# Pinning each engine to the staggered program order, and eight instead of six x and output buffers, in a matmul-mask-softmax kernel

## The chip, the cores and the metric

The kernel runs on one core of one Trainium2 chip. The metric is the device time of one execution in microseconds (us). A profiled execution also has a span, from its first to its last instruction, which is some 2 us shorter than the time. Executions of the kernel before fall into two groups: about 108.7 us, with a mean granted TensorE clock of 0.93, and about 110.8 us, with 0.91. (The granted clock is the share of its full clock that the profile records for TensorE.) Runs over 1.5% above the fastest of the same kernel are called slow. In the lines of the profile PE is TensorE, PEld its weight loads, DVE is VectorE, ACT ScalarE, POOL GpSimd and SP the engine that issues the transfers; L104 is line 104 of that kernel.

## The reference

```
batch, m, k, n = 16, 512, 512, 512
y = scale * np.matmul(x, weight)            # scale = 0.125
y = np.where(mask == 1, y, -1e9)            # mask = 1 strictly below the diagonal
y_max = np.max(y, axis=-1, keepdims=True)
y_exp = np.exp(y - y_max)
return (y_exp / np.sum(y_exp, axis=-1, keepdims=True)).astype(np.float32)
```

Sixteen batches of 512x512 in float32 are read and written: 1.049 MB in and 1.049 MB out for each. The weight and four diagonal blocks of the mask are read once.

## The kernel before

A batch goes through six steps. `load` fetches x. `cast` makes it bf16 on VectorE. `transpose` turns it on TensorE, by sixteen 128x128 transposes into PSUM, and evicts one half on VectorE and one on ScalarE. `multiply` makes four row tiles on TensorE, adds the mask through a matmul with the identity, and takes the exponential with its row sum on ScalarE. `normalise` multiplies by the reciprocal of the sums on VectorE. `store` writes out. `X_BUFS` and `OUT_BUFS` say how many x tiles (`xf`) and output tiles (`ot`) there are to take turns with; `xb` is x in bf16, `pt` its transpose in PSUM, `xt` the evicted transpose, `py` the product in PSUM. A tile framework makes the semaphores, and its scheduler may reorder the instructions of each engine.

```python
X_BUFS = 6
OUT_BUFS = 6
...
    def transpose(b):
        xb = st_xb.pop(b)
        xt = xt_pool.tile([P, KT, QT, P], BF16, name="xt")
        for half in range(2):
            pt = psum_t.tile([P, 2, QT, P], BF16, name="pt")
            for kk in range(2):
                ...                                   # eight transposes into pt
            if half == 0:
                nc.vector.tensor_copy(xt[:, 0:2], pt)  # "eviction"
            else:
                nc.scalar.copy(xt[:, 2:4], pt)
        st_xt[b] = xt
...
    for i in range(B + 1):
        if i + 2 < B:
            cast(i + 2)
        if i + 1 < B:
            transpose(i + 1)
        if i < B:
            multiply(i)
        if i >= 1:
            normalise(i - 1)
            store(i - 1)
            if i - 1 + X_BUFS < B:
                load(i - 1 + X_BUFS)
```

The softmax here doesn't subtract the row's maximum and nothing guards it: scores larger than these inputs give would overflow.

## Time and profile before

| | before |
|---|---|
| time, first three runs | 108.56, 110.81, 110.86 us (median 110.81) |
| span of the profiled execution | 106.9 us |
| bytes moved | 34.87 MB |
| busy: TensorE / VectorE / ScalarE | 68% / 53% / 50% |
| granted TensorE clock, mean | 0.932 |

No engine is near full, and the transfers move at 400 GB/s or more in 23 of the 40 slices and fall off in the last quarter. The prediction below shows the slices, the waits and one turn of the timeline. One line more is of use, from the waits of the queue that issues the transfers. Its columns are: who waits for whom, total us, times, longest us.

```profile
SPq L139 <- DVE ot L135: 77.7, 16, 8.5
```

All sixteen stores stand waiting for a normalisation. The longest wait, 8.5 us, is natural: it is that of the first store, before any batch is done. But after 50 us the queue still waits 46.1 us in eight times, up to 7.3 us for one store, when no load is late.

### The profile page before, as it was taken

To read this page: it belongs to the slowest core of one execution; us is meant where nothing else is said; L and a number is where in the kernel's file an instruction comes from. 1 tells how busy PE (TensorE), PEld (TensorE's weight loads), DVE (VectorE), ACT (ScalarE), POOL (GpSimd) and SP (SyncE) were. 2 spreads that over 40 slices of the span, in tenths; PEclk is the share of its full clock that TensorE was granted. 3 is DMA by queue.
4 is the path that set the end of the run, shared out by engine and by line. 5 is a ranking of instruction groups with operands and counts; after the bars stand their busy time and mean duration, and the time that the engine had idled before them with its cause. 6 is when DMAs were issued, how large, how long until landed. Compare 5 with 4: busy or idle time off the path is not lost. (4 is left out here: it accounts for less than half of the span.)

```text
span 106.9 us, 1599 instructions
## 1 busy us (share of the span) xinstructions
PE 73.2 (68%) x576; PEld 48.2 (45%) x576; DVE 57.0 (53%) x116; ACT 53.6 (50%) x147; POOL 14.9 (14%) x36
## 2 busy tenths in 40 slices
PE   0026994999999998937749669392992939929100
PEld 0025563685687665535535445362551626526000
DVE  0067329768987767788290390928409366070510
ACT  4007263696886874835613836375353563355300
POOL 7990001010410110110010100101001010010100
PEclk9999999999999999999975999999579996799975
DMA  2998999999999999999999999999950724505354
GB/s 28 400 382 282 422 417 411 406 411 417 369 296 371 415 400 420 415 420 418 418 423 420 415 418 418 420 425 420 412 204 14 294 98 193 199 0 239 153 222 170
DMA packets 9814, 34.95 MB, mean 327 GB/s; under 512 B 592, under 2 KB 1104, under 8 KB 9808
## 3 DMA queue, kind: packets, MB, share of 16 engines
q1 hardware_dynamic: 9808, 34.87, 82.4%
q8 instruction: 4, 0.07, 0.2%
q14 instruction: 2, 0.02, 0.0%
HBM read 18.09 MB, written 16.78 MB: 326 GB/s over the span
## 5 line engine op out<-in xcount | busy, mean ns | idle before, releaser
L104 PE MATMUL py<-w_bf,xt 128*128 128x256 bf16 (+1 forms) x256 | 56.6, 355 | 17.0 <-DVE xt L90 17.0
L119 ACT ACTIVATE ot<-py 128x256 f32<-128x256 f32 (+1 forms) x64 | 31.2, 491 | 31.5 <-PE py L111 31.0
L104 PEld LDWEIGHTS <-xt 128*128 128x128 bf16 x256 | 25.9, 105 | 33.8 <-DVE xt L90 19.2
L135 DVE TENSOR_SCALAR ot<-ot,rinv 128x256 f32<-128x256 f32 (+1 forms) x64 | 25.2, 438 | 1.6 <-issue 0.5
L77 DVE CAST xb<-xf 128x2048 bf16<-128x2048 f32 x16 | 20.1, 1257 | 7.4 <-DMA xf<-in_x_dram 7.4
L88 PE MATMUL pt<-ident_bf,xb 128*128 128x128 bf16 x256 | 17.8, 225 | 9.1 <-DVE xb L77 9.1
L88 PEld LDWEIGHTS <-xb 128*128 128x128 bf16 x256 | 16.0, 101 | 11.8 <-DVE xb L77 10.6
L132 DVE RECIPROCAL rinv<-rsum 128x4 f32<-128x4 f32 x16 | 2.8, 176 | 32.9 <-ACT ot L119 32.9
L92 ACT COPY xt<-pt 128x1024 bf16<-128x1024 bf16 x16 | 16.2, 1013 | 7.5 <-PE pt L88 4.0
L136 POOL MEMSET ot<- 1x256 f32 x16 | 7.8, 484 | 85.6 <-DVE ot L135 85.6
L111 PE MATMUL py<-diag_bf,ident_bf 128*128 128x256 bf16 x64 | 18.8, 294 | 0.0
L119 ACT ACTIVATION_READ_ACCUMULATOR ot<-py 128x1 f32 x64 | 12.7, 199 | 0.0
L90 DVE COPY xt<-pt 128x1024 bf16<-128x1024 bf16 x16 | 10.9, 680 | 1.5 <-PE pt L88 1.5
L111 PEld LDWEIGHTS <-ident_bf 128*128 128x128 bf16 x64 | 6.8, 106 | 5.1 <-issue 1.4
L168 ACT CAST w_bf<-w_f 128x512 bf16<-128x512 f32 x2 | 1.2, 622 | 6.7 <-DMA w_f<-in_weight_dram 6.7
L159 POOL MEMSET ot<- 128x512 f32 x6 | 3.0, 520 | 0.1
L160 POOL MEMSET ot<- 1x256 f32 x6 | 2.7, 481 | 0.0
L168 ACT ACT_TABLE_LOAD x1 | 1.3, 1283 | 0.7 <-PEq L208 0.7
L166 DVE CAST w_bf<-w_f 128x512 bf16<-128x512 f32 x2 | 0.8, 424 | 1.4 <-DMA w_f<-in_weight_dram 1.4
L170 DVE TENSOR_SCALAR diag_bf<-diag_f 64x512 bf16<-64x512 f32 x2 | 0.8, 416 | 0.0
L157 POOL MEMSET diag_bf<- 64x512 bf16 x1 | 0.5, 520 | 0.1
L156 POOL MEMSET diag_bf<- 64x512 bf16 x1 | 0.5, 523 | 0.0
(6 smaller groups left out, 0.9 us busy)
## 6 DMA issues: line engine op xcount, KB each, us to landing
xf<-in_x_dram SPq DMA_DIRECT2D x16, 1024.0 KB, 12.7
out_dram<-ot SPq DMA_DIRECT2D x16, 1024.0 KB, 9.2
w_f<-in_weight_dram SPq DMA_DIRECT2D x1, 1024.0 KB, 7.5
diag_f<-in_mask_dram SPq DMA_DIRECT2D x4, 64.0 KB, 6.7
```

What stands on the lines that cost most here:

```text
L77: nc.vector.tensor_copy(xb, st_x.pop(b))
L88: nc.tensor.transpose(pt[:, kk, q], xb[:, q, kt * P : (kt + 1) * P], ident_bf)
L90: nc.vector.tensor_copy(xt[:, 0:2], pt)
L92: nc.scalar.copy(xt[:, 2:4], pt)
L104: nc.tensor.matmul(py[:, :NC], lhsT=xt[:, kt, q], rhs=w_bf[:, kt, :NC], start=(kt == 0), stop=(kt == KT - 1),)
L111: nc.tensor.matmul(py[:, h * HB : NC], lhsT=ident_bf, rhs=diag_bf[:, q], start=False, stop=True, skip_group_check=True,)
L119: nc.scalar.activation(out=ot[:, q, :NC], in_=py[:, :NC], func=AF.Exp, bias=0.0, scale=float(scale), accum_out=rsum[:, q : q + 1],)
L132: nc.vector.reciprocal(rinv, st_sum.pop(b))
L135: nc.vector.tensor_scalar_mul(ot[:, q, :NC], ot[:, q, :NC], rinv[:, q : q + 1])
L136: nc.gpsimd.memset(ot[0:1, 0, :HB], 1.0 / N)
L159: nc.gpsimd.memset(ot[:, 0:2, HB:], 0.0)
L160: nc.gpsimd.memset(ot[0:1, 0, HB:], 1.0 / N)
```

## The change

The intent is to fix the order of every engine's instructions to the order of the program text, so that the scheduler can't move them. The pin is `keep_in_program_order`, which puts an instruction behind the one traced before it on the same engine. The text separates the evictions from the transposes, and both sets of buffers grow to eight.

```diff
-X_BUFS = 6
-OUT_BUFS = 6
+X_BUFS = 8
+OUT_BUFS = 8
...
+    seq = tc.keep_in_program_order
...
-        nc.vector.tensor_copy(xb, st_x.pop(b))
+        seq(nc.vector.tensor_copy(xb, st_x.pop(b)))
...                                   (the same seq(...) around every transfer, matmul,
...                                    activation, reciprocal, multiply and memset of a batch)
+    def evict(b):
         xt = xt_pool.tile([P, KT, QT, P], BF16, name="xt")
-        ... (transposes and evictions of each half in turn)
+        pt = st_pt.pop(b)
+        seq(nc.vector.tensor_copy(xt[:, 0:2], pt[0]))
+        seq(nc.scalar.copy(xt[:, 2:4], pt[1]))
         st_xt[b] = xt
...
     for i in range(B + 1):
+        if i + 1 < B:
+            transpose(i + 1)
         if i + 2 < B:
             cast(i + 2)
         if i + 1 < B:
-            transpose(i + 1)
+            evict(i + 1)
         if i < B:
             multiply(i)
```

More of the change, by code (lines that the diff above doesn't have):

```diff
@@ L66 @@
     ots = [const.tile([P, QT, N], FP32, name=f"ot{i}") for i in range(OUT_BUFS)]
-    st_x, st_xb, st_xt, st_sum = {}, {}, {}, {}
+    st_x, st_xb, st_pt, st_xt, st_sum = {}, {}, {}, {}, {}
+    seq = tc.keep_in_program_order
     def load(b):
         xf = x_pool.tile([P, QT, K], FP32, name="xf")
-        nc.sync.dma_start(xf.rearrange("p (h s) k -> p h (s k)", h=2), x_r[b])
+        seq(nc.sync.dma_start(xf.rearrange("p (h s) k -> p h (s k)", h=2), x_r[b]))
         st_x[b] = xf
@@ L81, in transpose @@
         xb = st_xb.pop(b)
-        xt = xt_pool.tile([P, KT, QT, P], BF16, name="xt")
-        for half in range(2):
-            pt = psum_t.tile([P, 2, QT, P], BF16, name="pt")
-            for kk in range(2):
-                kt = 2 * half + kk
-                for q in range(QT):
-                    nc.tensor.transpose(pt[:, kk, q], xb[:, q, kt * P : (kt + 1) * P], ident_bf)
-            if half == 0:
-                nc.vector.tensor_copy(xt[:, 0:2], pt)
-            else:
-                nc.scalar.copy(xt[:, 2:4], pt)
+        st_pt[b] = [psum_t.tile([P, 2, QT, P], BF16, name="pt") for _ in range(2)]
+        for kt in range(KT):
+            for q in range(QT):
+                seq(
+                    nc.tensor.transpose(
+                        st_pt[b][kt // 2][:, kt % 2, q],
+                        xb[:, q, kt * P : (kt + 1) * P],
+                        ident_bf,
+                    )
+                )
+    def evict(b):
+        xt = xt_pool.tile([P, KT, QT, P], BF16, name="xt")
+        pt = st_pt.pop(b)
+        seq(nc.vector.tensor_copy(xt[:, 0:2], pt[0]))
+        seq(nc.scalar.copy(xt[:, 2:4], pt[1]))
         st_xt[b] = xt
@@ L103, in multiply @@
             for kt in range(KT):
-                nc.tensor.matmul(
-                    py[:, :NC],
-                    lhsT=xt[:, kt, q],
-                    rhs=w_bf[:, kt, :NC],
-                    start=(kt == 0),
-                    stop=(kt == KT - 1),
-                )
-            nc.tensor.matmul(
-                py[:, h * HB : NC],
-                lhsT=ident_bf,
-                rhs=diag_bf[:, q],
-                start=False,
-                stop=True,
-                skip_group_check=True,
-            )
-            nc.scalar.activation(
-                out=ot[:, q, :NC],
-                in_=py[:, :NC],
-                func=AF.Exp,
-                bias=0.0,
-                scale=float(scale),
-                accum_out=rsum[:, q : q + 1],
+                seq(
+                    nc.tensor.matmul(
+                        py[:, :NC],
+                        lhsT=xt[:, kt, q],
+                        rhs=w_bf[:, kt, :NC],
+                        start=(kt == 0),
+                        stop=(kt == KT - 1),
+                    )
+                )
+            seq(
+                nc.tensor.matmul(
+                    py[:, h * HB : NC],
+                    lhsT=ident_bf,
+                    rhs=diag_bf[:, q],
+                    start=False,
+                    stop=True,
+                    skip_group_check=True,
+                )
+            )
+            seq(
+                nc.scalar.activation(
+                    out=ot[:, q, :NC],
+                    in_=py[:, :NC],
+                    func=AF.Exp,
+                    bias=0.0,
+                    scale=float(scale),
+                    accum_out=rsum[:, q : q + 1],
+                )
             )
@@ L131, in normalise @@
         rinv = sum_pool.tile([P, QT], FP32, name="rinv")
-        nc.vector.reciprocal(rinv, st_sum.pop(b))
+        seq(nc.vector.reciprocal(rinv, st_sum.pop(b)))
         for q in range(QT):
             NC = (q // 2 + 1) * HB
-            nc.vector.tensor_scalar_mul(ot[:, q, :NC], ot[:, q, :NC], rinv[:, q : q + 1])
-        nc.gpsimd.memset(ot[0:1, 0, :HB], 1.0 / N)
+            seq(nc.vector.tensor_scalar_mul(ot[:, q, :NC], ot[:, q, :NC], rinv[:, q : q + 1]))
+        seq(nc.gpsimd.memset(ot[0:1, 0, :HB], 1.0 / N))
     def store(b):
-        nc.sync.dma_start(out_r[b], ots[b % OUT_BUFS].rearrange("p (h s) n -> p h (s n)", h=2))
+        seq(nc.sync.dma_start(out_r[b], ots[b % OUT_BUFS].rearrange("p (h s) n -> p h (s n)", h=2)))
     load(0)
-    nc.sync.dma_start(w_f32, weight.rearrange("(kt p) n -> p kt n", p=P))
+    seq(nc.sync.dma_start(w_f32, weight.rearrange("(kt p) n -> p kt n", p=P)))
     for h in range(2):
@@ L147 @@
             r = h * HB + g * P
-            nc.sync.dma_start(
-                diag_f32[g * HP : (g + 1) * HP, 2 * h : 2 * h + 2],
-                mask[r : r + P, r : r + P].rearrange("(p s) c -> p s c", s=2),
+            seq(
+                nc.sync.dma_start(
+                    diag_f32[g * HP : (g + 1) * HP, 2 * h : 2 * h + 2],
+                    mask[r : r + P, r : r + P].rearrange("(p s) c -> p s c", s=2),
+                )
             )
@@ L163 @@
     transpose(0)
+    evict(0)
     for kt in range(KT):
         if kt % 2 == 0:
-            nc.vector.tensor_copy(w_bf[:, kt], w_f32[:, kt])
+            seq(nc.vector.tensor_copy(w_bf[:, kt], w_f32[:, kt]))
         else:
-            nc.scalar.copy(w_bf[:, kt], w_f32[:, kt])
+            seq(nc.scalar.copy(w_bf[:, kt], w_f32[:, kt]))
     for g in range(2):
-        nc.vector.tensor_scalar(
-            out=diag_bf[g * HP : (g + 1) * HP, :, g * P : (g + 1) * P],
-            in0=diag_f32[g * HP : (g + 1) * HP],
-            scalar1=-MASK_NEG,
-            scalar2=MASK_NEG,
-            op0=ALU.mult,
-            op1=ALU.add,
+        seq(
+            nc.vector.tensor_scalar(
+                out=diag_bf[g * HP : (g + 1) * HP, :, g * P : (g + 1) * P],
+                in0=diag_f32[g * HP : (g + 1) * HP],
+                scalar1=-MASK_NEG,
+                scalar2=MASK_NEG,
+                op0=ALU.mult,
+                op1=ALU.add,
+            )
         )
```

## The prediction

> **What bounds the kernel now.** I began with the page's slices, because they show at once that there are two regimes.
>
> ```profile
> PE   0026994999999998937749669392992939929100
> DVE  0067329768987767788290390928409366070510
> PEclk9999999999999999999975999999579996799975
> DMA  2998999999999999999999999999950724505354
> GB/s 28 400 382 282 422 417 411 406 411 417 369 296 371 415 400 420 415 420 418 418 423 420 415 418 418 420 425 420 412 204 14 294 98 193 199 0 239 153 222 170
> ```
>
> A slice is 106.9 / 40 = 2.67 us. Up to slice 29 (about 78 us) the DMA engines run at 400 to 425 GB/s, but for a dip to 296 in slices 10 to 12. In the last 29 us the rate is mostly below 240. The windows view gives the means (columns: busy us and instructions of each engine, granted TensorE clock, DMA share, GB/s):
>
> ```profile
> 26.00:34.00 8.00, 8.00 (x75) 5.81 (x72) 6.94 (x15) 5.97 (x19) 1.77 (x2) 1.00 0.98 344
> 34.00:54.00 20.00, 16.16 (x142) 10.74 (x140) 13.08 (x30) 13.09 (x38) 2.10 (x5) 1.00 1.02 416
> 54.00:74.00 20.00, 13.98 (x108) 9.25 (x108) 10.56 (x23) 9.80 (x27) 1.34 (x3) 0.91 1.02 419
> 77.50:107.00 29.50, 15.96 (x115) 9.78 (x113) 10.91 (x25) 11.18 (x31) 1.79 (x4) 0.85 0.41 162
> ```
>
> The waits then say who holds up whom (total us, times, longest):
>
> ```profile
> DVE rinv L132 <- ACT ot L119: 32.9, 13, 4.2
> PE py L104 <- DVE xt L90: 17.0, 10, 1.9
> DVE xb L77 <- DMA xf<-in_x_dram: 7.4, 2, 5.7
> ```
>
> The casts wait for a load only twice, for the first two batches. So no later load is late: compute runs behind the loads, the loads (six buffers deep) are finished at 78 us, and five batches are left to compute with nothing to load. One period of that tail in the timeline (start us, busy us, instruction, idle before):
>
> ```profile
> 82.29 0.83 PE L104 MATMUL py<-w_bf,xt 128*128 128x256 bf16 x6 [1.93 <-DVE xt L90]
> ...
> 85.34 1.06 PE L88 MATMUL pt<-ident_bf,xb 128*128 128x128 bf16 x16
> 85.54 0.60 ACT L119 ACTIVATE ot<-py 128x512 f32<-128x512 f32 x1 [0.28 <-PE py L111]
> ...
> 86.53 1.14 DVE L135 TENSOR_SCALAR ot<-ot,rinv 128x256 f32<-128x256 f32 x3
> ...
> 87.60 0.67 DVE L90 COPY xt<-pt 128x1024 bf16<-128x1024 bf16 x1
> 88.19 0.47 DVE L135 TENSOR_SCALAR ot<-ot,rinv 128x512 f32<-128x512 f32 x1
> 88.33 0.86 PE L104 MATMUL py<-w_bf,xt 128*128 128x256 bf16 x6 [1.93 <-DVE xt L90]
> ```
>
> The multiply starts at 82.29, the next batch's transposes stand behind it, and VectorE takes reciprocal and three normalising multiplies of the old batch before it evicts the new transposes at 87.60. Only then can the next multiply start, at 88.33. This ring is 88.33 - 82.29 = 6.04 us per batch, with 1.9 us of idle TensorE. **The bound is an ordering ring, not an engine.**
>
> **What the Trainium skill says.** "Perfetto Trace Analysis", section Optimization Strategy, says that a kernel can have several regimes with a different most-contended engine, and that interleaving the regimes can help. The trace agrees: 416 to 419 GB/s for forty microseconds, then 162. "DMA: Bandwidth & Descriptors", section Where 436 GB/s comes from, puts the ceiling of a core's transfers at 435 GB/s. The saturated windows here hold 414 to 419, so I use the measured rates. "TensorE: Matmul & The Clock Gate", Part 1, says that TensorE has a full and a half clock, chosen by activity over windows of about 3.4 us, idleness giving the half clock. The trace has both: the clock row falls to 5, and the ring then lasts longer (next multiply at 96.04, so 7.71 us). But the longest wait of the multiplies is 1.9 us, so here less than a fully idle window was enough. The same Part 1 says that VectorE and ScalarE queues are strictly first in, first out, which is why program order matters; the ring above, where an eviction stands behind a normalisation, agrees.
>
> **The change, part by part.** No arithmetic is added. Two ot buffers add two 128x512 memsets of 0.52 us and two small ones on GpSimd, before first use and off the path.
>
> *Order.* Each turn becomes, on TensorE: transposes of i+1, multiply of i; on VectorE: cast of i+2, eviction of i+1, normalisation of i-1; on ScalarE: eviction of i+1, exponentials of i. The instruction order of the built kernel shows just this on every engine. Multiply i now needs only an eviction of the turn before, so the ring is cut. What remains is each engine's own work. The trace already has a stretch where the scheduler chose nearly such an order:
>
> ```profile
> 26.62 0.60 PE L104 MATMUL py<-w_bf,xt 128*128 128x256 bf16 x4
> ...
> 30.55 0.60 PE L104 MATMUL py<-w_bf,xt 128*128 128x256 bf16 x4
> ```
>
> That is 30.55 - 26.62 = 3.93 us per batch with TensorE always busy: 16 transposes from 29.66 to 30.55 (0.89) and a multiply of about 3.04. VectorE starts its pieces in that stretch at distances of 0.61 (eviction), 0.20 (reciprocal), 1.46 (normalise) and 1.15 (cast), in all 3.42. ScalarE has 1.01 for its eviction, 2 x 0.37 and 2 x 0.58 for exponentials, in all 2.9. So compute can go at 3.93 us per batch. The DMA needs 2 x 1.049 MB / 417 GB/s = 5.03 us per batch. **DMA becomes the bound.**
>
> *Buffers.* The dip of slices 10 to 12 comes when six loads have landed and stores are still few (the second store is issued at 26.12). With eight x buffers two more loads, 2 x 2.5 = 5 us of transfer, stand in the queue. The second load lands at 12.64 (its cast waits for it); six more at 2.54 us bring the eighth to about 27.9. When is the first store? Turn 0 now puts the transposes of batch 1 first: cast 12.64 to 13.87, transposes at the cold clock 1.9 us to 15.8, multiply 0 some 4 us (half cold) to 19.8, transposes of batch 2 to 20.7, eviction 21.4, normalisation 1.8, store at about 23.4. That is 5 us later than the 18.24 of before, but ahead of 27.9, so the queue does not run dry.
>
> *The sum.* From the slices, 2.67 x (28 + 400 + 382 + 282) kB plus 1.95 us at 422 GB/s, 3.74 MB have moved by 12.64 us. In all 34.87 MB must move (18.09 read, 16.78 written). Up to the last load: 34.87 - 3.74 - 8 stores of 1.049 = 22.74 MB at 416 GB/s = 54.7 us, so 67.3. Then eight stores alone, 8.39 MB. A lone store shows 401 to 410 GB/s in the windows of the last transfer, say 405: 20.7 us, so 88.0. After its last bytes (before 105.5) the kernel before ran on to 106.9, another 1.4: span 89.4. The profiled run took 108.95 us for a span of 106.9, so 2.05 more: **91.5 us**.
>
> Does compute keep up? First store 23.4, then 3.93 per batch, less the 0.9 of transposes that the last turn lacks: the last store is issued at about 81.5. The last load lands at 67.3, and the cast of batch 15 comes by the same pace (some 42 us after the cast of batch 4 at 23.3) at 66.5, so it waits about a microsecond. The queue needs the last store by 88.0 - 2.6 - 1.6 = 83.8. Slack is some 2 us, or 0.15 us per batch. That is thin, and it is why my centre stands half a microsecond above the sum: **92.0 us**.
>
> **The rivals.** *Compute stays the bound* at a pace above 4.1 us. For it: slack is thin, VectorE is 87% loaded at 3.93 us, and the clock can fall when TensorE starts to wait for loads. Against it: the 3.93 stretch was measured with DMA saturated around it and the clock at 1.00. At 4.4 us per batch the last store is at 88.5, and the time is about 96. *The late start costs:* turn 0 waits for the second load before multiply 0. If the first store came after 28 us, the DMA would idle for the difference; 3 us more makes 95. *The transfers were hidden anyway, so nothing is gained:* true of the two buffers alone in the first 78 us, but not of the tail of 29 us at 162 GB/s, so I reject it for the whole. *In-order blocking:* VectorE waits at a late cast and holds a ready normalisation, hence a store and a load. It could starve the queue only if fewer transfers stood in it than the wait is long; up to eight are in flight here (each transfer in the built order waits for the eighth before it), so the loss should be nil.
>
> **Range and chances.** The floor is all bytes at 424 GB/s, the best window, with stores too: 31.13 MB / 424 = 73.4 us after 12.64, plus 1.4 and 2.05, or 89.5. The slow rivals reach 96. Eight in ten: 89.7 to 96.5. Faster by over 2% means under 108.6; only a return of the ring would prevent it. Chances 0.97, 0.02, 0.01.
>
> **What would show it.** Right: the GB/s row above 400 from slice 2 nearly to the last, no dip near 27 us, first store near 23 us, turns of 3.9 us up to about 60 us, casts of late batches waiting for loads, the multiply's wait for an eviction gone from the list, last store issued near 82 us with several stores still queued. Wrong: DMA holes in the last quarter with TensorE at clock 0.5 (compute bound), a hole before 30 us (late start), or a store-only rate well below 405.

## The result

| | before | changed |
|---|---|---|
| time, median | 109.81 us (108.56 to 110.86, 4 runs) | 92.25 us (92.04 to 92.59, 4 runs) |
| span, profiled execution | 106.9 us | 90.1 us |
| mean rate over the span | 327 GB/s | 388 GB/s |

The ratio is 0.849 (95% interval 0.844 to 0.854). A ratio here is the mean time of one kernel's fast runs over that of the other's of the same rounds, so it isn't quite the ratio of the medians.

The slices of the changed kernel, each 90.1 / 40 = 2.25 us:

```profile
PE   0007108999999999999999999999999999400000
DVE  0055744669797897979789778678493998450000
PEclk9999999999999999999999999999999999996555
GB/s 15 360 355 307 390 415 413 413 407 411 409 407 418 420 422 420 422 405 405 422 420 420 424 407 418 422 413 429 411 424 409 425 416 425 416 424 420 420 313 20
```

The rate holds from slice 4 to slice 37. TensorE is full from 13.9 us until it has nothing left at about 77.5 us, and its clock falls only afterwards. Two turns of TensorE (start us, busy us, instruction) answer to the two lines of the ring before:

```profile
27.07 1.06 PE L87 MATMUL pt<-ident_bf,xb 128*128 128x128 bf16 x16
27.97 0.60 PE L111 MATMUL py<-w_bf,xt 128*128 128x256 bf16 x4
...
31.00 1.06 PE L87 MATMUL pt<-ident_bf,xb 128*128 128x128 bf16 x16
```

A turn is 31.00 - 27.07 = 3.93 us, with no wait in it. The waits, in the form of before:

```profile
DVE xb L78 <- DMA xf<-in_x_dram: 14.5, 8, 5.6
PE pt L87 <- DVE xb L78: 12.0, 2, 7.4
DVE rinv L144 <- ACT ot L130: 1.5, 2, 1.2
```

The multiplies' wait for an eviction (17.0 us before) is gone, and the reciprocals' wait for the exponentials fell from 32.9 to 1.5 us. The casts now wait for loads eight times instead of twice. The two waits of the transposes are those of the start. Late in the run (VectorE's timeline) a cast looks like this:

```profile
69.15 1.23 DVE L78 CAST xb<-xf 128x2048 bf16<-128x2048 f32 x1 [1.40 <-DMA xf<-in_x_dram]
```

This is the last batch. Compute has caught up with the transfers. The windows of the last 23 us show that after this the transfers go on without compute (columns as in the prediction):

```profile
54.00:74.00 20.00, 20.00 (x182) 14.26 (x181) 15.00 (x32) 15.86 (x46) 1.92 (x5) 1.00 1.03 419
...
80.00:86.00 6.00, 0.00 (x0) 0.00 (x0) 0.14 (x1) 0.00 (x0) 0.00 (x0) 0.64 1.03 421
```

From 80 to 86 us the queue only drains stores, at 421 GB/s.

One caution on reading. The changed kernel's chain of work that ended last is laid to TensorE for 71% of the span. That view follows one possible chain back from the last instruction, and it passes through a TensorE that was always busy. It doesn't show that a shorter TensorE would end sooner. Run e5_no_diag tests that.

### The profile page after: what moved, and what is told of

Read it like the earlier page. It is cut to its first block, busy times and chain, and to the rows that moved or that the text cites. A ratio compares the mean times of both kernels' runs of the same rounds, so it can differ in the third digit from the quotient of the medians.

```text
span 90.1 us, 1605 instructions
## 1 busy us (share of the span) xinstructions
PE 65.6 (73%) x576; PEld 47.3 (52%) x576; DVE 57.4 (64%) x116; ACT 52.8 (59%) x147; POOL 15.7 (17%) x40
## 4 chain that ended last, share of the span: by engine, by line
PE 71%; DMA 9%; SPq 4%; DVE 3%; ACT 1%; issue 1%; DVEq 0%; ACTq 0%
PE py L111 47%; PE pt L87 16%; DMA xf<-in_x_dram 9%; PE py L120 8%; SPq L161 3%; DVE ot L147 1%; DVE xb L78 1%; ACT ot L130 1%; SPq L155 1%; SPq L73 0%; DVEq L241 0%; DVE rinv L144 0%; ACTq L241 0%; DVEq L147 0%
## 5 line engine op out<-in xcount | busy, mean ns | idle before, releaser
L111 PE MATMUL py<-w_bf,xt 128*128 128x256 bf16 (+1 forms) x256 | 50.0, 329 | 0.0
L111 PEld LDWEIGHTS <-xt 128*128 128x128 bf16 x256 | 24.7, 99 | 11.5
L87 PE MATMUL pt<-ident_bf,xb 128*128 128x128 bf16 x256 | 18.6, 231 | 12.0 <-DVE xb L78 12.0
L147 DVE TENSOR_SCALAR ot<-ot,rinv 128x256 f32<-128x256 f32 (+1 forms) x64 | 24.5, 446 | 1.0
L87 PEld LDWEIGHTS <-xb 128*128 128x128 bf16 x256 | 16.9, 104 | 14.3 <-DVE xb L78 12.6
L120 PE MATMUL py<-diag_bf,ident_bf 128*128 128x256 bf16 x64 | 17.6, 275 | 0.0
L120 PEld LDWEIGHTS <-ident_bf 128*128 128x128 bf16 x64 | 6.3, 99 | 4.2
L173 POOL MEMSET ot<- 128x512 f32 x8 | 3.9, 519 | 0.1
```

The lines of the kernel that those rows point to most:

```text
L87: nc.tensor.transpose(st_pt[b][kt // 2][:, kt % 2, q], xb[:, q, kt * P : (kt + 1) * P], ident_bf,)
L111: nc.tensor.matmul(py[:, :NC], lhsT=xt[:, kt, q], rhs=w_bf[:, kt, :NC], start=(kt == 0), stop=(kt == KT - 1),)
L120: nc.tensor.matmul(py[:, h * HB : NC], lhsT=ident_bf, rhs=diag_bf[:, q], start=False, stop=True, skip_group_check=True,)
L147: seq(nc.vector.tensor_scalar_mul(ot[:, q, :NC], ot[:, q, :NC], rinv[:, q : q + 1]))
L173: nc.gpsimd.memset(ot[:, 0:2, HB:], 0.0)
```

## The experiments

**What the builds alone showed.** A build gives the order of each engine's instructions without a run. When the changed kernel is built with the old loop text (cast, then transposes and evictions together) but pinned, every engine gets exactly the same instruction sequence as in the changed kernel. So the old text already stated the staggered order, and splitting off the evictions changes nothing once the pins hold. In the kernel before, the scheduler departs from it. Its build has the ring (reciprocal and three normalising multiplies of batch b ahead of the eviction of b+1, all multiplies of b ahead of the transposes of b+1) for b = 7 to 14, which is eight turns.

**Order alone.** Edit: the changed kernel with `X_BUFS = OUT_BUFS = 6`.

```diff
-X_BUFS = 8
-OUT_BUFS = 8
+X_BUFS = 6
+OUT_BUFS = 6
```

> The pinned order with six x and six output buffers as before. Theory (the order is what gains, the buffers only bridge the late first store): first store near 22.3 us as in the changed kernel, sixth load landed near 23.0, so a hole of about 1.2 us in the transfers near 23 to 24 us and nothing else; 93.4 us (92.8 to 94.5). Rival (the buffers carry a good part of the gain): 97 us or more, with casts waiting for loads from the sixth batch on.

Measured: 96.51 us (95.57 to 96.56), 0.884 of before. The direction was right, the size was not: it is 3.1 us over the expected value and nearer to the rival's 97. The order alone takes 12.2 us off the 108.7 of before, and the two buffers on top of it another 4.3. The windows of this run show where:

```profile
22.00:23.00 1.00, 1.00 (x10) 0.78 (x8) 0.96 (x5) 1.00 (x3) 0.45 (x1) 1.00 0.09 33
23.00:24.00 1.00, 1.00 (x7) 0.49 (x5) 1.00 (x3) 0.69 (x5) 0.00 (x0) 1.00 0.06 16
...
26.50:27.00 0.50, 0.47 (x4) 0.28 (x3) 0.50 (x2) 0.50 (x3) 0.43 (x1) 1.00 0.99 238
27.00:27.50 0.50, 0.47 (x3) 0.24 (x3) 0.50 (x2) 0.50 (x4) 0.00 (x0) 1.00 1.03 221
27.50:28.00 0.50, 0.50 (x5) 0.25 (x4) 0.50 (x2) 0.24 (x2) 0.00 (x0) 1.00 0.94 213
```

The queue is empty from 22 to 24.5 us, because the first store was issued at 23.75 us here and not at 22.3. Most of that delay is a slower start of TensorE: its first multiply took from 15.91 to 20.68 us, 4.77, where the changed kernel's took 3.66 (15.55 to 19.21). In both, the first matmuls are slow (1.06 us for four of 256 columns, later 0.60), here for longer, which the clock row doesn't show (1.00). The runs with four and five buffers below started as slowly, the other profiles of a staggered order with eight did not; why is open. Once transfers resumed they moved at 311 to 401 GB/s for 2 us, and then at only 213 to 238 for 1.5 us. By the windows from 22 to 32 us, 2.55 MB moved where 416 GB/s would have moved 4.16, a loss of 1.61 MB or 3.9 us. That is most of the 4.3 us by which this run is longer than the changed kernel. A second, smaller hole, which the expectation didn't have either, lies at the end: from 81 to 83 us the rate is 176 and 258 GB/s, about 1 us lost, because fewer stores stand in the queue when the last batches are computed. The low rate near 27 us comes where a lone store gives way to a lone load. The run with four buffers shows the same in its turns (205 and 180 GB/s from 50 to 51 us); lone stores in the tail of before, with no load behind them, don't (410, 418, 385 and 410 GB/s from 90 to 92 us). Why, no run here tells. The casts wait for loads from the seventh batch on, which is what the rival said, but that is only what being bound by transfers looks like.

**Buffers alone.** Edit: the kernel before with eight and eight.

```diff
-X_BUFS = 6
-OUT_BUFS = 6
+X_BUFS = 8
+OUT_BUFS = 8
```

> The kernel before with eight x and eight output buffers, the scheduler free to order. Theory: compute is bound by the ordering ring, which buffers do not touch, so 107 to 111 us, within 2% of before, with turns of 6.0 us (7.7 at the low clock) in the second half; the dip of the transfer rate near 28 us is gone. Rival (buffers carry a good part): below 103 us.

Measured: 99.13 to 99.24 us in three fast runs, 101.9 in a slow one; 0.911 of before. This was a clear miss: the buffers alone, with a free scheduler, took 10 us. But the builds differ in more than the buffers. With eight, the ring stands in the order only for batches 10 to 14, five turns instead of eight. (Built with eight x buffers and six output buffers, the ring also begins at batch 10, in a milder form; with six x and eight output buffers it stands where it stood before. So it is the x buffers that move the scheduler.) The rate and the windows of this run agree:

```profile
34.00:54.00 20.00, 19.81 (x179) 13.98 (x179) 15.23 (x34) 15.14 (x45) 2.97 (x5) 1.00 1.03 418
54.00:74.00 20.00, 14.11 (x120) 9.76 (x122) 13.30 (x28) 11.54 (x34) 1.79 (x4) 1.00 1.02 419
74.00:96.90 22.90, 11.16 (x79) 6.84 (x78) 7.46 (x18) 8.09 (x24) 1.34 (x3) 0.84 0.61 246
```

TensorE is full until 54 us, and then the ring begins. In the kernel before it was busy for 16.16 of the 20 us from 34 to 54. Three turns fewer at 6.04 - 3.93 = 2.1 us make 6.3 us. The rest may be the low clock: turns of 7.7 us in place of 6.0 come three times in the tail of before (to 60.45, 80.23 and 93.98, by the gaps of its reciprocals) and once in this run (to 83.97), and two of them are 3.3 us. The last experiment below separates order from buffers.

**The ring, pinned.** Edit: the changed kernel with the loop in the order of the ring.

```diff
-    for i in range(B + 1):
-        ... (the staggered turn)
+    for i in range(B):
+        multiply(i)
+        if i + 1 < B:
+            transpose(i + 1)
+        normalise(i)
+        if i + 1 < B:
+            evict(i + 1)
+        if i + 2 < B:
+            cast(i + 2)
+        store(i)
+        if i + X_BUFS < B:
+            load(i + X_BUFS)
```

> Eight buffers and every instruction pinned, but in the order of the ring: multiply i, transposes of i+1, normalise i, evict i+1, cast i+2. Theory (the staggered order gains, pinning as such does not): the ring is 6.04 us plus the fourth normalising multiply ahead of the eviction, 6.4 us at the full clock and 8.1 at the low one, so 115 to 128 us. Rival (pinning itself, by taking disorder away, gains): about 92 us.

Measured: 125.83 and 127.32 us in the two fast runs, 130.46 in two slow ones; the ratio is 1.162. Eight buffers and pins, with the ring in every turn, are 16% slower than the free scheduler with six, which has it in eight. The pin has no merit of its own; the last experiment shows this again, with the very order of before.

**The text without the pins.** Edit: `seq` does nothing.

```diff
-    seq = tc.keep_in_program_order
+    seq = lambda ins: ins
```

> The changed kernel with the pins taken out and nothing else: eight buffers, the new text, the scheduler free. The build shows the ring (reciprocal and three normalising multiplies ahead of the eviction) again from about the eighth batch on. Theory (the pins are what holds the order): 103 to 110 us. Rival (the rewritten text, with its separate evict, suffices): 92 to 94 us.

Measured: 101.44 us (101.34 to 102.06), 0.933 of before. That lies outside the rival and just under the expected range. The builds, compared once more, say why: without the pins the new text gives every engine exactly the instructions of "buffers alone", with the ring for batches 10 to 14 (and not from about the eighth, as the expectation has it). So this is a second measurement of that kernel, and the 2.2 us between 99.2 and 101.4 are not of the text. The profile there has one turn at the low clock (7.72 us to 83.97), here there are two (7.71 us each, to 78.35 and 92.09), with mean clocks of 0.961 and 0.939; the slow run there, 101.9 us, had 0.942. Of the change, 7 us (with fast runs) to 9 us hang on the pins.

**The place of the eviction on VectorE.** Edit: the normalisation (with its store and load) moves ahead of the cast and the eviction.

```diff
         if i + 1 < B:
             transpose(i + 1)
+        if i >= 1:
+            normalise(i - 1)
+            store(i - 1)
+            ... (load)
         if i + 2 < B:
             cast(i + 2)
         if i + 1 < B:
             evict(i + 1)
         if i < B:
             multiply(i)
-        ... (normalise, store, load)
```

> The changed kernel with VectorE's turn as normalise i-1, cast i+2, evict i+1 in place of cast, evict, normalise. Theory (what matters is that transposes of i+1 stand ahead of multiply i on TensorE and that the normalisation is of an older batch, not the place of the eviction on VectorE): the eviction ends about 3.9 us after the transposes begin, still ahead of the next multiply at 3.93 + 0.89, so 92.3 us (91.8 to 93.5). Rival (an eviction behind a normalisation is itself the loss, since TensorE waits for it): each turn grows by the normalisation's 1.7 us, so 105 us or more.

Measured: 91.88 us (91.81 to 92.43). An eviction that stands behind a normalisation of an older batch costs nothing. What the ring lost by was that the normalisation was of the batch just multiplied, with the transposes behind that same multiply.

**Are the transfers now the bound?** Three runs on one chip. First, less TensorE work. Edit: the mask matmuls are left out, so the results are wrong.

```diff
-            seq(
-                nc.tensor.matmul(
-                    py[:, h * HB : NC],
-                    lhsT=ident_bf,
-                    rhs=diag_bf[:, q],
-                    start=False, stop=True, skip_group_check=True,
-                )
-            )
```

> The changed kernel without the 64 mask matmuls (wrong results on purpose). It takes 4 x 0.107 = 0.43 us off TensorE's turn, 3.93 to 3.50, all transfers kept. Theory (transfers bound the changed kernel): unchanged, 92.25 us within 0.5. Rival (TensorE, whose chain the profile names for 71% of the span, is the bound): 92.25 - 15 x 0.43 = 85.8 us.

Measured: 92.46 us (92.32 to 92.57). The time didn't move, so TensorE isn't the bound, whatever the chain says. VectorE's timeline keeps the pace of the changed kernel:

```profile
64.09 1.23 DVE L78 CAST xb<-xf 128x2048 bf16<-128x2048 f32 x1 [1.48 <-DMA xf<-in_x_dram]
...
69.03 1.23 DVE L78 CAST xb<-xf 128x2048 bf16<-128x2048 f32 x1 [1.40 <-DMA xf<-in_x_dram]
```

The casts come 69.03 - 64.09 = 4.94 us apart, at the pace of the loads, and the last one begins at 69.03 as against 69.15 with the mask matmuls. The saved time turns up as waiting: TensorE now waits for a cast six times (17.5 us), where it did so twice (12.0 us).

Second, more TensorE work. Edit: the transposes of two of the four column blocks are done twice, with right results.

```diff
-        for kt in range(KT):
+        for kt in (0, 1, 0, 1, 2, 3):
```

> The changed kernel with eight of the sixteen transposes of each batch done twice (same values, right results): 8 x 0.056 = 0.45 us more of TensorE per turn, 3.93 to 4.38. Theory (transfers bound it, compute has some 3.6 us of slack at the end: last store issued at 80.2, 4.2 us for its own transfer, last bytes at about 88): last store at 80.2 + 16 x 0.45 = 87.4, its bytes end at 91.6, so 3.6 us later, 95.9 us (94.5 to 97). Rival (compute is the bound already): 92.25 + 7.2 = 99.4. Rival (much slack): 92.3.

Measured: 94.48 us (94.39 to 95.74), 2.2 us more than the changed kernel for 16 x 0.45 = 7.2 us more of TensorE. So some 5 us were slack, where 3.6 had been expected. The end of its windows shows compute as the bound:

```profile
84.00:85.00 1.00, 0.45 (x3) 0.07 (x1) 0.00 (x0) 0.71 (x4) 0.00 (x0) 1.00 0.10 41
...
87.00:88.00 1.00, 0.00 (x0) 0.00 (x0) 0.02 (x1) 0.00 (x0) 0.00 (x0) 1.00 0.59 234
88.00:89.00 1.00, 0.00 (x0) 0.00 (x0) 0.00 (x0) 0.00 (x0) 0.00 (x0) 0.96 0.99 406
```

The queue runs low near 80 us (135 GB/s from 80 to 81), dry near 84 and again near 87 us, and waits for stores. In the changed kernel it never did.

Third, the transfers alone, in the same order, the stores taking constant tiles (wrong).

```diff
-    cast(0)
-    ... (all compute)
+    for i in range(1, B + 1):
+        store(i - 1)
+        if i - 1 + X_BUFS < B:
+            load(i - 1 + X_BUFS)
```

> Only the transfers of the changed kernel in the same order on the same queue, the stores taking constant tiles and waiting for no compute (wrong results on purpose). Theory (the changed kernel is at the floor of its transfers): 91.3 to 92.4 us, with 413 to 420 GB/s until the end. Rival (compute costs transfers time, by late stores or contention): 89 us or less.

Measured: 90.61 us (90.48 to 90.64 in the timed runs; the profiled one took 91.64). This is a little below the expected range, between it and the rival, and is taken here as the floor for this list of transfers. (Its stores start at 13.0 us, as they wait for no compute.) The two kernels with compute on the same chip, e4 and e5, took 91.88 and 92.46. So with compute the kernel stands 1.3 to 1.9 us, or 1.4 to 2%, above its transfers. The spans of the timed runs, 88.7 to 88.9 us for the transfers alone and 89.9 to 90.5 for e4, put some 1.1 us of it inside the span. Where it lies is not settled: only the profiled run leaves a trace, and that of the transfers alone was its slowest, with a span of 89.9.

**Taking a transfer away.** If transfers bind, then fewer of them must help, even at the start. Edit: the mask tile is made on GpSimd in place of the four mask loads (64 KB each, in 512-byte packets) and the work on them. This takes the mask's strictly lower triangular form for granted. The kernel skips blocks by the same assumption, but until now it took the values in the diagonal blocks from the input.

```diff
-            seq(nc.sync.dma_start(diag_f32[...], mask[r : r + P, r : r + P]...))   # four of them
-    ... (two memsets and two multiply-adds that turn diag_f32 into diag_bf)
+    nc.gpsimd.memset(diag_bf, 0.0)
+    for q in range(QT):
+        nc.gpsimd.affine_select(
+            out=diag_bf[:, q], in_=diag_bf[:, q],
+            compare_op=ALU.is_gt, fill=MASK_NEG, base=q % 2,
+            pattern=[[-1, HB]], channel_multiplier=2,
+        )
```

> The changed kernel with the mask tile made on GpSimd from the triangular form that the program assumes anyway, in place of four loads of 64 KB in 512-byte packets and the work on them. Theory (transfers bound it, and those small packets cost 1.0 to 1.6 us of transfer time, as the rate falls to 214 GB/s near 8.5 us): 90.8 us (90.3 to 91.4). Rival (the start is hidden behind compute): 92.25 within 0.3.

Measured: 90.96 us (90.75 to 91.51), with right results, 0.840 of before (0.836 to 0.843), as against 0.849 for the changed kernel. It is the fastest correct version. Against the changed kernel that is 1.0 us by the ratios (0.009 of 108.7) and 1.3 by the medians, from different chips. The mask is 0.26 MB, 0.63 us at 416 GB/s, so its loads cost about one and a half to two times what their bytes would.

**How few buffers the pinned order bears.** Edit: four, and five, of each.

```diff
-X_BUFS = 8
-OUT_BUFS = 8
+X_BUFS = 4
+OUT_BUFS = 4
```

> The pinned order with four x and four output buffers. Theory of in-order blocking: store b is issued 3.6 us after cast b+3 begins, and load b+n stands behind it and lands some 6.6 us later, so cast b+n cannot begin sooner than 10.2 us after cast b+3. With n = 4 that is 10.2 us a batch: 12 x 10.2 plus 29 plus 13, about 160 us (140 to 170), slower than before by far. Rival (fewer buffers only bring back the hole at the start): 97 to 100 us.

Measured: 174.99 us (174.49 to 175.48), 1.61 times before. The timeline of VectorE:

```profile
42.84 1.23 DVE L78 CAST xb<-xf 128x2048 bf16<-128x2048 f32 x1 [7.78 <-DMA xf<-in_x_dram]
43.98 0.68 DVE L97 COPY xt<-pt 128x1024 bf16<-128x1024 bf16 x1
44.58 0.17 DVE L144 RECIPROCAL rinv<-rsum 128x4 f32<-128x4 f32 x1
44.79 1.53 DVE L147 TENSOR_SCALAR ot<-ot,rinv 128x256 f32<-128x256 f32 x4
54.04 1.23 DVE L78 CAST xb<-xf 128x2048 bf16<-128x2048 f32 x1 [7.72 <-DMA xf<-in_x_dram]
```

The mechanism is as expected, a cast that holds the normalisation behind it and with it the next load. The turn is 54.04 - 42.84 = 11.2 us, not 10.2: the store is issued at 46.39 and the load at 46.82, and the load lands 7.2 us after its issue, where 6.6 after the store's had been put in. The missing microsecond is about what the low rate between store and load costs (319, 188, 205 and 180 GB/s from 49 to 51 us). With this turn the same sum gives 29 + 12 x 11.2 + 13 = 176 us.

> The pinned order with five buffers of each. By the same rule two batches share 10.2 us, 5.1 us a batch, a hair above the transfers' 5.03: about 96 us (94 to 101). Rival (only the start suffers): 94 us or less.

Measured: 109.15 and 107.61 us in the two fast runs (109.41 and 110.11 in slow ones), not 96. The same term was too small: two batches share 11.2 us, so 5.6 us each and not 5.1, and later casts in its profile come 5.2 to 6.5 us apart. To this comes a hole at the start, which the hand sum had left out: its slices 7 and 8 (19 to 24 us) move 90 and 6 GB/s. With five, the pinned order is worth nothing against before (ratio 1.000). With six the same rule gives 11.2 / 3 = 3.7 us, under the 5.03 of the transfers, and no longer binds.

**The old order with eight buffers.** The miss of e2_buffers_only left open whether buffers or order gave its 10 us. Edit: the kernel before with eight buffers, each engine pinned to the very sequence that its build with six has. The build was compared with that of before and agrees on TensorE, VectorE and ScalarE instruction for instruction; the queue of transfers has two loads more at its head, and GpSimd the memsets of two more tiles.

```diff
-X_BUFS = 6
-OUT_BUFS = 6
+X_BUFS = 8
+OUT_BUFS = 8
...
-    for i in range(B + 1):
-        ... 
+    for word in ORDER.split():          # the 814 operations, in an order that keeps
+        op, *at = word.split(",")       # each engine's sequence of the kernel before
+        ops[op](*map(int, at))          # each op pinned with keep_in_program_order
```

> The kernel before, with eight x and eight output buffers, but every engine pinned to the instruction order that the build of the kernel before has with six. The builds show why this is asked: with six buffers the scheduler puts the ring into 8 turns (batches 7 to 14), with eight into 5 (batches 10 to 14), in an otherwise alike text. Theory (buffers gained 10 us in the free order only because the scheduler then chose a better order): 107.5 to 109.5 us in fast runs, as before with six. Rival (the buffers themselves, through transfers or slots, give the gain): 99 to 101 us.

Measured: 108.2 us (the three fast runs 107.72 to 108.35, a slow one 110.83), ratio 0.994 (0.987 to 1.001). Its waits and its rate:

```profile
PE py L152 <- DVE xt L142: 16.9, 10, 1.9
```

```profile
GB/s 28 398 369 302 420 418 409 409 409 406 418 420 418 420 415 406 422 422 420 420 422 422 415 415 420 420 422 420 344 144 0 320 76 213 182 0 245 150 230 165
```

The wait of the multiplies is as before (17.0, 10, 1.9), and so is the tail. The dip of before at slices 10 to 12 is filled, which is worth 0.6 us by the mean of the fast runs, and by the interval between nothing and 1.4 us. So it was the order. The two buffers, by themselves, do nothing for the old order that is clear of the noise. They gained in the free kernel because the scheduler then made a better order. Why it does so isn't shown by any run.

The four corners together:

| | six buffers | eight buffers |
|---|---|---|
| scheduler free | about 108.7 (fast) | 99.2 (the same build again: 101.4) |
| order of the ring as built with six, pinned | not run | 108.2 |
| staggered order, pinned | 96.5 | 92.25 |

## Why the prediction was right, point by point

- **The bound before is an ordering ring.** Held. Pinned with eight buffers it gives 108.2 us again, and a purer form of it 126 us. The staggered order removed the multiplies' wait for evictions. (The "five batches" left at 78 us are four: of the six stores from 68.94 us on, two were issued before that.)
- **The pace of compute, 3.93 us.** Held to the second decimal: 31.00 - 27.07. It lasts until casts begin to wait for loads, at 54.26 us and not at about 60; then turns are 4.9 to 5.0 us.
- **The first store at 23.4 us, before the queue is empty at 27.9.** It was issued at 22.29, and there is no hole near 27 us. The margin matters: with six buffers, and a first store at 23.75 us, the hole cost 3.9 us. How long TensorE runs slow at the start isn't in the prediction's control, so part of the margin is luck.
- **The transfers become the bound.** Held: with 0.43 us less TensorE work per turn nothing changed, and the transfers alone took 90.6.
- **The last load at 67.3 us.** The cast of the last batch waited until 69.15, so this was 1.9 us too early. By then, estimated from 3.8 MB at 12.58 us (its slices) and 416 GB/s since, 27.3 MB had moved, not 26.5: stores queued behind the last load had begun to move before it had landed. So the delay cost nothing. (The prediction's "some 42 us" from the cast of batch 4 to that of batch 15 is 11 x 3.93 = 43.2; its 66.5 rests on the right value.)
- **Eight stores alone at 405 GB/s.** Stores in a full queue ran at 421; 405 was the rate of a lone one. For the 7.5 MB that were left at 69.15 us this is 0.7 us less.
- **The end.** Span 89.4 predicted, 90.1 measured. The rate falls off slowly from 86.5 us (369, 188, 156, 41 and 8 GB/s in half-microseconds), where the kernel before stopped short, and the time is 1.9 to 2.5 us above the span, not 2.05. These two, less what the faster stores gave, are the 0.75 us between the sum of 91.5 and the 92.25 measured. The half microsecond that was added for the thin slack was not needed for that; it covered this. So it is luck that 92.0 came within 0.3 us; the sum itself was 0.75 us off.
- **Slack of some 2 us in compute.** Too small: 7.2 us more of TensorE cost 2.2, so it was about 5. The last store was issued at 80.2 us, not 81.5.
- **The rival "nothing is gained, transfers were hidden anyway", said to be true of the two buffers alone.** It is true for a given order (108.2), but not for the kernel as a whole: a free scheduler answers to the buffer count, and took 10 us from it. The prediction had not asked what the count does to the order.
- **Under 108.6 us as faster by 2%.** This was taken from a median of 110.81 us that two slow runs had made; from the fast runs of before it is 106.5. Here it decides nothing.
- **In-order blocking loses nothing with up to eight transfers in flight.** Held at eight. At four it makes the kernel 1.6 times as slow as before.

## What to carry to other kernels

When no engine and no queue is full, look for a ring: one turn of the timeline, read from a wait back to the same wait, shows which instruction stands in front of another without need. Before crediting a change of buffers, compare the instruction order of the two builds, since a scheduler may answer to a buffer count with another order; and two texts may give one and the same build. And an order pinned on in-order engines needs enough buffers: an instruction that waits for a load holds all behind it, among them the store and the next load.

## What the Trainium skill lacked or had wrong

- "TensorE: Matmul & The Clock Gate", Part 1, lets the clock fall after an idle window of about 3.4 us; its passage on a second failure mode has short idle times between groups of matmuls do the same, but gives no length. In the kernel before the clock fell to 0.50 three times in turns of the ring, for 3.41 us each, although the multiplies' longest wait was 1.9 us: in the 3.41 us before each fall TensorE was busy for some 1.48. That isn't a threshold: in the run of buffers alone the same 1.48, from 68.91 to 72.32 us, was followed by no fall.
- No page has what happens where a lone 1 MB store gives way to a lone 1 MB load. Here a lone store moved at 401 to 410 GB/s in mid-transfer, but at that change the rate was 213 to 238 GB/s for some 1.5 us with six buffers, and 180 to 205 for as long with four (49.5 to 51 us), with the DMA engines shown as 82% busy or more.
